# A retention head scales its values behind the third bank copy, and its rows are put together one unit later

## The chip, the cores and the metric

The kernel runs on one core of a Trainium2 chip. The metric is the device time of one execution in microseconds (us), the median of several runs. Beside it there is a profile of one execution.

## The reference

One layer of a decoder trunk: an RMS norm, one input projection into eight parts, a gated short convolution on four of them, retention on the other four, an output projection and a final RMS norm, all in fp32. Sixteen meta tokens stand ahead of the 2048 positions.

```python
D_MODEL, SEQ, N_META = 1024, 2048, 16      # D_CONV = D_RET = 512, 4 heads of 128

def short_conv_branch(h, b_gate, c_gate, conv_w):
    u = c_gate * h
    conv = causal_depthwise_conv(u, conv_w)             # width 3
    return b_gate * conv

def mixer_layer(h, norm_g, w_in, conv_w, ret_norm_g, w_out, pos):
    hn = rms_norm(h, norm_g)
    cx, cb, cc, cg, q, k, v, rg = jnp.split(hn @ w_in, 8, axis=-1)
    conv_out = short_conv_branch(cx, cb, cc, conv_w) * jax.nn.silu(cg)
    ...
    ret = head_group_norm(retention_chunkwise(rotary(q) * 128 ** -0.5, rotary(k), v), ret_norm_g)
    ret_out = ret * jax.nn.silu(rg)
    return h + jnp.concatenate([conv_out, ret_out], axis=-1) @ w_out

def reference(x, meta, ...):
    h = jnp.concatenate([meta, x], axis=1)
    h = mixer_layer(h, ...)
    return rms_norm(h, final_g)[:, N_META:]
```

`retention_chunkwise` works in chunks of 128 positions: masked scores q k^T times v inside a chunk, plus q times a 128x128 state carried from chunk to chunk with a fixed decay.

## The kernel before

**Rounds, units, quads.** The 2048 positions are done in two rounds of 1024 (two halves of 512). A round has eight units: four heads (0 to 3) and four conv groups (4 to 7), in the order of `UNITS`: round 0 begins with conv group 4 without the fast products, then heads 0 to 3, then 5 to 7; round 1 has heads 0 to 3 and then 4 to 7. After them come the output products. Each unit has two quads: a first one (k and v of a head, two of the conv's parts) and a second one (q and the gate rg, or the other two parts). A quad multiplies a 2x2 block of weights (blocks of 512 rows by 128 columns) with a 2x2 block of the moving rows by seven products (0 to 6) instead of eight. One product is 12 matmuls of L236: four slices of 128 rows, each as three matmuls, because each operand is split into a high part (`wh`, `mh`) and a rest (`wl`, `ml`). ACT casts `wh` (L112), DVE subtracts to get `wl` (L113), with three buffers of each. The sums of weight blocks that the seven products need are made in place by POOL (`sa`, `ra`: L121, L124, L151).

**Banks, copies and steps.** The products write into three PSUM banks: 0, 2, 4, 6 into `xb`, 1 into `yb`, 3 and 5 into `zb`. ACT copies a bank out (L243) after products 0, 2 and 3; these are the first, second and third bank copies, and product 5 overwrites the bank of the third. After each copy, `step()` calls the next of the quad's `steps`, whose instructions are to be placed behind that copy. `take` uses the finished banks on DVE.

**A head's second quad.** The matmuls of the retention need k and v turned from columns to rows. That is a transpose by DMA on 16-bit halves: a copy into planes by `part` (L678 on ACT, `pl`), the DMA (L671, `tr`), and a copy back (`v` by L766, `kd` by L757). The values `v` are then scaled by four small ACT instructions (L769), a factor for each chunk. Behind the first copy of the quad stand the splits of v and of half 0's k; behind the second `join(0)` (copy back and scaling of half 0's values) and the split of half 1's k; behind the third `join_keys(0)`; behind the quad the same for half 1. Then come the matmuls of the states (L798), the scores (L811, masked by DVE at L813 into `pm`) and the output (L821, L822), spread over the next unit's first quad.

**Turning the result.** A head's normalised output is turned back in two stages, each kept in `waiting`. Stage 0 (`turn`): ACT's copy L844, a transpose by DMA, silu of the gate (L847). It runs behind the first quad of the next unit. Stage 1 (`finish`), for each half of 512: ACT's copy L850 (`apart`), one product on DVE with gain and gate (L851, `qg`), and the store of the rows to DRAM (L506). `catch_up(1)` runs it behind the second quad of that next unit.

**What sets the order.** A scheduler gives each engine one fixed order of instructions when the kernel is built. It follows data and buffers, and the places that the code asks for with `issue_after`. In round 0, matmuls for the meta tokens (L456, L486, L494) are placed between those of the projection. SP issues nearly all DMAs, one queue in order: weight loads (L498), transposes (L671), stores (L506), and blocks of `w_out` with their sums (L427, L205).

Of the kernel before, what the change touches and what calls it, by code (L numbers as in the profile page):

```python
# [78 lines left out]
def hybrid_trunk(ctx: ExitStack, tc: tile.TileContext, t, out: bass.AP, chunk_decay):  # L79
# [5 lines left out]
    nc = tc.nc  # L85
# [40 lines left out]
    def load_raw(loads):  # L126
        tiles = []
        for load in loads:
            a = raw()
            load(a)  # L130
            tiles.append(a)
        return tiles
# [3 lines left out]
    def stationary(blocks):  # L136

        a11, a12, a21, a22 = blocks
        s1 = sb.tile([P, HB], F32, name="sa", tag="ra", bufs=RAW)

        def parts(src):
            hi = sb.tile([P, HB], F32R, name="wh", tag="wh", bufs=RING)
            lo = sb.tile([P, HB], F32R, name="wl", tag="wl", bufs=RING)
            split(hi, lo, src)
            return hi, lo

        w = [parts(a11), parts(a12)]
        add(nc.gpsimd, s1, a21, a22)
        sub(nc.gpsimd, a21, a11, a21)
        sub(nc.gpsimd, a11, s1, a11)  # L150
        summed[0] = nc.gpsimd.tensor_tensor(out=a12, in0=a12, in1=a11, op=ALU.subtract)  # L151
        w += [parts(a) for a in (a11, s1, a21)]
        fifth[0] = lowered[0]
        return w + [parts(a) for a in (a12, a22)]
# [70 lines left out]
    def quad(w, m, take, steps=()):  # L225


        steps = iter(steps)

        def product(i, bank, first):  # L230
            (wh, wl) = w[i]
            for kt in range(KH):
                ks = slice(kt * P, (kt + 1) * P)
                mh, ml = m[i][kt]
                for n, (a, b) in enumerate(((wl, mh), (wh, ml), (wh, mh))):
                    nc.tensor.matmul(  # L236
                        bank, a[:, ks], b, start=first and kt == 0 and n == 0, stop=kt == KH - 1 and n == 2,
                        skip_group_check=not first,
                    )

        def copy(bank):
            c = sb.tile([P, HB], F32, name="tc", tag="tc", bufs=COPIES)
            copied[0] = nc.scalar.copy(out=c, in_=bank)  # L243
            return c

        def step():
            with tc.issue_after(copied[0].ins):
                next(steps, lambda: None)()

        xb = ps_proj()  # L250
        product(0, xb, True)
        c = copy(xb)
        step()
        yb = ps_proj()
        product(1, yb, True)
        take(0, 0, yb, c)
        product(2, xb, False)
        u2 = copy(xb)
        step()
        zb = ps_proj()  # L260
        product(3, zb, True)
        c = copy(zb)
        step()
        product(4, xb, False)
        take(1, 1, xb, c)
        product(5, zb, False)
        take(0, 1, zb, u2)
        product(6, xb, False)
        take(1, 0, xb, None)
# [89 lines left out]
    def raw():  # L359
        return sb.tile([P, HB], F32, name="ra", tag="ra", bufs=RAW)  # L360
# [136 lines left out]
    def w_loads(n):  # L497
        return [lambda a, i=i: nc.sync.dma_start(a, t["w_in"][n, i]) for i in range(4)]  # L498
# [83 lines left out]
    def conv_group(g, r, m, f, blocks, ahead, steps=(), last=False):  # L582


        def go_on():
            next(factors_ahead[0], None)

        def behind(quad, *own):
            return [lambda n=n: (own[n](), go_on() if (quad, n) in steps else None) for n in range(3)]

        u = [gen("u") for _ in range(2)]
        rr, rr2 = ([a[:, j * HB : (j + 1) * HB] for j in range(2)] for a in f[:2])
        held = [None]

        def mul(eng, out, a, b):
            eng.tensor_tensor(out=out, in0=a, in1=b, op=ALU.mult)  # L596

        def take(i, j, pp, c):
            s = u[j][:, 2:]
            if c is None:  # L600
                mul(nc.vector, s, pp, s)
            elif i == 1:
                add(nc.vector, c, pp, c)
                held[0] = c
            else:
                add(nc.vector, s, pp, c)
                mul(nc.vector, s, s, rr2[j])
                if j == 1:
                    mul(nc.gpsimd, s, s, held[0])

        blocks, meta = blocks
        quad(stationary(blocks), m, take, behind(0, idle, idle, idle))
        catch_up(0)
        if meta:
            meta_carry(g, meta)
        carry(u, g, r)
        cs = [taps(u[j], g) for j in range(2)]
        gates = []

        def gated():  # L620
            j, c = gates.pop()
            nc.scalar.activation(c, c, AF.Silu)  # L622
            mul(nc.gpsimd, cs[j], cs[j], rr[j])
            mul(nc.gpsimd, cs[j], cs[j], c)

        def take(i, j, pp, c):
            if i == 0:
                add(nc.vector, c, pp, c)
                mul(nc.vector, c, c, rr[j])
                gates.append((j, c))  # L630
                if j == 1:
                    gated()
                return
            if c is not None:
                add(nc.vector, c, pp, c)
                pp = c
            taken[0] = nc.vector.tensor_tensor(out=cs[j], in0=pp, in1=cs[j], op=ALU.mult)  # L637

        n = 2 * (NG + g) + 1
        quad(stationary(load_raw(w_loads(n))), m, take, behind(1, idle, gated, idle))  # L640
        catch_up(1)
        blocks = ahead()
        def store():
            for j in range(2):
                store_mixed(r, j, g, cs[j])

        if last:
            kept.append(store)
        else:
            store()  # L650
        return blocks
# [12 lines left out]
    def halves(a):  # L664
        return a.bitcast(U16).rearrange("p (n two) -> p two n", two=2)

    def planes(a):
        return a.bitcast(U16).rearrange("p (two n) -> p two n", two=2)
# [16 lines left out]
    waiting = [[], []]  # L685

    def catch_up(stage):


        if waiting[stage]:  # L690
            with tc.issue_after(copied[0].ins):
                while waiting[stage]:
                    waiting[stage].pop(0)()

    def head(h, r, m, rot_t, f, turning, blocks, ahead, sums, first=(), between=((), idle, idle)):


# [3 lines left out]
        k, v, late = [None, None], [None, None], []  # L701
# [19 lines left out]
        if len(first) > 0:  # L721
            quad_plain(first[0], m, take)
        else:
            quad(stationary(blocks[0]), m, take, between[0])
            catch_up(0)
        between[1]()
        if to_cross:
# [27 lines left out]
        def join_keys(j):  # L755
            kt[j] = brief("kd")
            nc.scalar.copy(out=halves(kt[j]), in_=planes(across_k[j]))  # L757
# [6 lines left out]
        def join(j):  # L764
            a = gen("v")[:, :HB]
            nc.scalar.copy(out=halves(a), in_=planes(v[j]))  # L766
            for c in range(CH):
                cs = slice(c * P, (c + 1) * P)
                nc.scalar.mul(a[:, cs], a[:, cs], f[2][j][0][:, h, c : c + 1])  # L769
            v[j] = a  # L770

        def middle():
            join(0)
            split_keys(1)

        quad(stationary(load_raw(w_loads(2 * h + 1))), m, take, (split_late, middle, lambda: join_keys(0)))
        catch_up(1)
        with tc.issue_after(copied[0].ins):
            join(1)
            join_keys(1)  # L780
        between[2]()
        with tc.issue_after(queried[0].ins):
# [4 lines left out]
        with tc.issue_after(loaded[0].ins) if len(first) else nullcontext():  # L787
            blocks = ahead()
        states = [state[h]]
        vt = []  # L790
        for j in range(2):
# [4 lines left out]
            for c in range(CH - last):  # L796
                cs = slice(c * P, (c + 1) * P)
# [9 lines left out]
        for j in range(2):  # L807
            sc = ps_misc()
            for c in range(CH):
                cs = slice(c * P, (c + 1) * P)  # L810
# [8 lines left out]
            for c in range(CH):  # L819
                cs = slice(c * P, (c + 1) * P)  # L820
# [15 lines left out]
            for c in range(CH):  # L836
                cs = slice(c * P, (c + 1) * P)
# [133 lines left out]
    for r in range(NR):  # L971
        f = factors[r]
# [6 lines left out]
        if r == 0:  # L979
# [3 lines left out]
            def begin(half):  # L983
# [21 lines left out]
            m, b = moving(  # L1005
                load_x(r), gain_of, {(0, 0): lambda: begin(0), (0, KH - 1): lambda: begin(1), (0, KT - 1): normalise_meta}
            )
            first = [[p for a, p in w]]
            blocks = None, meta_products([a for a, p in w])
# [21 lines left out]
            between = (), idle, idle  # L1031
            later = prepare(load_x(1), sums_x, gain_of)
        else:
            m, b = moving(load_x(r), gain_of)
# [9 lines left out]
            between = (), rest_of_sums, idle  # L1044
            blocks = None, None
# [5 lines left out]
        for n, unit in enumerate(units):  # L1051
            following = units[n + 1] if n + 1 < len(units) else None
            rest = lambda: ahead(r, following, early=n == 0)
            if r + n == 0:
                blocks, completion = group_plain(unit - NG, m, f, blocks[1], first, late_parts, rest)
                special = (), completion
            elif unit < NG:
# [3 lines left out]
                blocks = head(unit, r, m, rot_t, f, turning, blocks, rest, sums, *(special if unit == 0 else ()))  # L1061
            else:
# [8 lines left out]
                blocks = conv_group(unit - NG, r, m, f, blocks, rest, FACTOR_STEPS.get(unit, ()) if r == 0 else (), r == 0 and following is None)  # L1071
# [4 lines left out]
    m, b = moving(load_w_out)  # L1076
# [42 lines left out]
```

## Time and profile before

| what | value |
|---|---|
| time, median of 3 runs | 870.76 us (869.86 to 871.42) |
| profiled execution, its time | 871.07 us |
| its span, first to last instruction | 869.3 us |
| granted TensorE clock | 0.998 |
| DMA | 129.51 MB, mean 149 GB/s |

Lines of the page's groups read: source line, engine, operation, output<-inputs, count | busy us in all, mean ns of one | idle us of the engine ahead of them and what ended it. Lines of the timeline read: start in us from the span's start, duration, engine, line, operation, operands, count, and in brackets idle time ahead of it with what ended it. PEld is the weight load of TensorE. Matmul durations overlap, since they are pipelined: the distance between two starts is what one costs. Lines of the view of waits read: the waiting engine and line, what it waited for, us in total, times, longest us.

### The profile page before, as it was taken

To read this page: it belongs to the slowest core of one execution; us is meant where nothing else is said; L and a number is where in the kernel's file an instruction comes from. 1 tells how busy PE (TensorE), PEld (TensorE's weight loads), DVE (VectorE), ACT (ScalarE), POOL (GpSimd) and SP (SyncE) were. 2 spreads that over 40 slices of the span, in tenths; PEclk is the share of its full clock that TensorE was granted. 3 is DMA by queue.
4 is the path that set the end of the run, shared out by engine and by line. 5 is a ranking of instruction groups with operands and counts; after the bars stand their busy time and mean duration, and the time that the engine had idled before them with its cause. 6 is when DMAs were issued, how large, how long until landed. Compare 5 with 4: busy or idle time off the path is not lost.

```text
span 869.3 us, 12705 instructions
## 1 busy us (share of the span) xinstructions
PE 857.9 (99%) x4216; PEld 704.7 (81%) x4216; DVE 722.5 (83%) x1194; ACT 497.9 (57%) x899; POOL 396.6 (46%) x286
## 2 busy tenths in 40 slices
PE   9999999999999999999999999999999999999996
PEld 6878887878787878788888888888888888788885
DVE  6899988888897977989789898988767799867663
ACT  8676548383845554848383747553333566545553
POOL 0663332322246654352233333355645445677773
PEclk9999999999999999999999999999999999999999
DMA  9724336363656633845264656647122584545441
GB/s 332 226 80 97 76 82 164 106 171 110 136 192 186 202 98 97 306 155 146 61 139 140 130 161 121 206 109 218 49 78 78 171 327 133 167 162 179 160 134 73
DMA packets 127219, 129.51 MB, mean 149 GB/s; under 512 B 58353, under 2 KB 75569, under 8 KB 127153
## 3 DMA queue, kind: packets, MB, share of 16 engines
q1 hardware_dynamic: 126576, 128.30, 50.0%
q8 instruction: 33, 0.54, 0.3%
q10 hardware_dynamic: 576, 0.40, 0.1%
q14 instruction: 34, 0.27, 0.1%
HBM read 90.91 MB, written 25.17 MB: 134 GB/s over the span
## 4 chain that ended last, share of the span: by engine, by line
PE 86%; DVE 3%; ACT 3%; issue 1%; DMA 1%; SPq 0%; POOLq 0%; POOL 0%; ACTq 0%; DVEq 0%
PE pj L236 73%; PE pj L293 5%; PE ms L822 2%; PE ms L811 2%; PE ms L821 2%; PE ms L798 2%; DVE ml L113 1%; PE ms L456 1%; ACT v L769 1%; ACT wh L112 1%; ACT v L766 1%; DVE wl L113 1%; DMA w<-in_w_out 1%; ACT tc L243 1%; DVE yo L121 0%
## 5 line engine op out<-in xcount | busy, mean ns | idle before, releaser
L236 PE MATMUL pj<-mh,wl 128*128 128x512 f32 x1008 | 397.2, 394 | 1.5 <-ACT tc L243 0.8
L236 PE MATMUL pj<-mh,wh 128*128 128x512 f32 x1008 | 393.0, 390 | 0.0
L236 PE MATMUL pj<-ml,wh 128*128 128x512 f32 x1008 | 392.7, 390 | 0.0
L112 ACT CAST wh<-ra 128x512 fp32r<-128x512 f32 x216 | 133.8, 620 | 245.2 <-PE pj L236 209.6
L113 DVE TENSOR_TENSOR wl<-ra,wh 128x512 fp32r<-128x512 f32 x216 | 194.4, 902 | 40.8 <-ACT wh L112 39.9
L236 PEld LDWEIGHTS pj<-mh,wl 128*128 128x128 f32 x1008 | 189.3, 188 | 45.5 <-ACT tc L243 3.9
L236 PEld LDWEIGHTS pj<-mh,wh 128*128 128x128 f32 x1008 | 189.3, 188 | 39.7
L236 PEld LDWEIGHTS pj<-ml,wh 128*128 128x128 f32 x1008 | 189.3, 188 | 37.5
L121 POOL TENSOR_TENSOR sa<-ra 128x512 f32<-128x512 f32 x36 | 53.0, 1473 | 104.7 <-DMA ra<-in_w_in 39.5
L124 POOL TENSOR_TENSOR ra<-sa,ra 128x512 f32<-128x512 f32 x36 | 53.9, 1497 | 91.8 <-DVE wl L113 88.8
L124 POOL TENSOR_TENSOR ra<-ra 128x512 f32<-128x512 f32 x36 | 59.1, 1643 | 49.4 <-PE ms L456 28.1
L151 POOL TENSOR_TENSOR ra<-ra 128x512 f32<-128x512 f32 x36 | 60.2, 1673 | 46.9 <-issue 37.1
L243 ACT COPY tc<-pj 128x512 f32<-128x512 f32 x108 | 62.7, 580 | 0.1
L293 PE MATMUL pj<-mh,mh 128*128 128x512 f32 x128 | 51.1, 400 | 0.7 <-ACT mh L115 0.6
L293 PE MATMUL pj<-mh,ml 128*128 128x512 f32 x128 | 50.1, 391 | 0.9 <-DVE ml L113 0.9
L293 PE MATMUL pj<-ml,mh 128*128 128x512 f32 x128 | 48.0, 392 | 0.0
L834 POOL TENSOR_TENSOR rp<-rs,neg_half 128x4 f32<-128x4 f32 x16 | 18.9, 1184 | 38.5 <-DVE rs L121 38.4
L596 POOL TENSOR_TENSOR c<-c,rr 128x512 f32<-128x512 f32 x14 | 24.9, 1778 | 24.3 <-DVE c L637 15.6
L897 DVE TENSOR_TENSOR yo<-pj,yo 128x512 f32<-128x512 f32 (+1 forms) x33 | 22.0, 671 | 16.2 <-PE pj L236 8.4
L908 POOL TENSOR_TENSOR z<-yo,final_g 128x512 f32<-128x512 f32 x16 | 26.8, 1675 | 18.6 <-DVE yo L897 18.6
L596 POOL TENSOR_TENSOR c<-c,tc 128x512 f32<-128x512 f32 x14 | 24.2, 1732 | 21.9 <-ACT tc L622 16.3
L112 ACT CAST wh<-sa 128x512 fp32r<-128x512 f32 x36 | 22.2, 617 | 15.0 <-PE pj L236 14.6
(153 smaller groups left out, 1218.9 us busy)
## 6 DMA issues: line engine op xcount, KB each, us to landing
ra<-in_w_in SPq DMA_DIRECT2D x126, 256.0 KB, 2.8
x<-in_xT SPq DMA_DIRECT2D x48, 256.0 KB, 4.9
w<-in_w_out SPq DMA_DIRECT2D x32, 256.0 KB, 4.7
ra<-mixed SPq DMA_DIRECT2D x32, 256.0 KB, 2.9
yo<-in_x SPq DMA_DIRECT2D x32, 256.0 KB, 4.9
ra<-in_x SPq DMA_DIRECT2D x16, 256.0 KB, 3.7
mixed<-c SPq DMA_DIRECT2D x16, 256.0 KB, 2.5
mixed<-qg SPq DMA_DIRECT2D x16, 256.0 KB, 2.4
```

What stands on the lines that cost most here:

```text
L112: nc.scalar.copy(out=hi, in_=src)
L113: lowered[0] = eng.tensor_tensor(out=lo, in0=src, in1=hi.bitcast(F32), op=ALU.subtract)
L121: eng.tensor_tensor(out=out, in0=a, in1=b, op=ALU.add)
L124: eng.tensor_tensor(out=out, in0=a, in1=b, op=ALU.subtract)
L151: summed[0] = nc.gpsimd.tensor_tensor(out=a12, in0=a12, in1=a11, op=ALU.subtract)
L236: nc.tensor.matmul(bank, a[:, ks], b, start=first and kt == 0 and n == 0, stop=kt == KH - 1 and n == 2, skip_group_check=not first,)
L243: copied[0] = nc.scalar.copy(out=c, in_=bank)
L293: nc.tensor.matmul(banks[i], a[:, ks], b, start=half + kt + n == 0, stop=half == 1 and kt == KH - 1 and n == 2,)
L596: eng.tensor_tensor(out=out, in0=a, in1=b, op=ALU.mult)
L834: nc.gpsimd.tensor_tensor(out=rp, in0=rs, in1=neg_half.rearrange("p (c a) -> p c a", a=1), op=ALU.pow)
L897: last[0] = nc.vector.tensor_tensor(out=y[:, cs], in0=pp[:, cs], in1=y[:, cs], op=ALU.add)
L908: nc.gpsimd.tensor_tensor(out=ys[i][j], in0=y, in1=final_g[:, j * HB : (j + 1) * HB], op=ALU.mult)
```

## The change

Two things are changed. A head's `join(0)` no longer scales half 0's values; the new `weigh(0)` does that behind the third bank copy instead of ahead of it, before `join_keys(0)`. And `catch_up(1)` is gone from the second quads of heads and conv groups; a new `finish_late` runs the waiting `finish` calls behind the first bank copy of the first quad of the unit after that. All instructions stay; a few lines move their numbers by some lines.

```diff
@@ conv_group
-        quad(stationary(blocks), m, take, behind(0, idle, idle, idle))
+        quad(stationary(blocks), m, take, behind(0, finish_late, idle, idle))
         catch_up(0)
...
         quad(stationary(load_raw(w_loads(n))), m, take, behind(1, idle, gated, idle))
-        catch_up(1)
@@
+    def finish_late():
+        while waiting[1]:
+            waiting[1].pop(0)()
@@ head
-            quad(stationary(blocks[0]), m, take, between[0])
+            quad(stationary(blocks[0]), m, take, between[0] or (finish_late,))
             catch_up(0)
...
         def join(j):
             a = gen("v")[:, :HB]
             nc.scalar.copy(out=halves(a), in_=planes(v[j]))
+            v[j] = a
+
+        def weigh(j):
             for c in range(CH):
                 cs = slice(c * P, (c + 1) * P)
-                nc.scalar.mul(a[:, cs], a[:, cs], f[2][j][0][:, h, c : c + 1])
-            v[j] = a
+                nc.scalar.mul(v[j][:, cs], v[j][:, cs], f[2][j][0][:, h, c : c + 1])
...
+        def late_middle():
+            weigh(0)
+            join_keys(0)
+
-        quad(stationary(load_raw(w_loads(2 * h + 1))), m, take, (split_late, middle, lambda: join_keys(0)))
-        catch_up(1)
+        quad(stationary(load_raw(w_loads(2 * h + 1))), m, take, (split_late, middle, late_middle))
         with tc.issue_after(copied[0].ins):
             join(1)
+            weigh(1)
             join_keys(1)
```

ACT, second quad of round 1's head 1, from the scalings ahead of the third bank copy (the first L243) to the cast ahead of the next unit's first one, before:

```order
L769 ACTIVATE v<-v,vk 128x128 x4
L112 CAST wh<-ra 128x512
L243 COPY tc<-pj 128x512
L757 COPY kd<-tr 128x2x512
L850 COPY apart<-across 128x2x512 x2
L112 CAST wh<-ra 128x512
L757 COPY kd<-tr 128x2x512
L112 CAST wh<-ra 128x512
L766 COPY v<-tr 128x2x512
L112 CAST wh<-ra 128x512
L769 ACTIVATE v<-v,vk 128x128 x4
L112 CAST wh<-sa 128x512
```

The same stretch now, and on to the next unit's first bank copy (the second L243) and the rows behind it. L766 is now L769, L769 is L775, L757 is L760, L850 is L859:

```order
L112 CAST wh<-ra 128x512
L243 COPY tc<-pj 128x512
L775 ACTIVATE v<-v,vk 128x128 x4
L760 COPY kd<-tr 128x2x512
L112 CAST wh<-ra 128x512
L760 COPY kd<-tr 128x2x512
L112 CAST wh<-ra 128x512 x2
L769 COPY v<-tr 128x2x512
L775 ACTIVATE v<-v,vk 128x128 x4
L112 CAST wh<-sa 128x512
L243 COPY tc<-pj 128x512
L859 COPY apart<-across 128x2x512 x2
```

The four scalings of half 0 stand behind the third copy, and the two copies of rows are out of this quad and in the next.

DVE, first quad of conv group 6 in round 0, around the `wl` of products 3 (from `sa`) and 4 (the next L113), before and now (L851 is now L860):

```order
L113 TENSOR_TENSOR wl<-sa,wh 128x512
L121 TENSOR_TENSOR u<-pj,tc 128x512
L113 TENSOR_TENSOR wl<-ra,wh 128x512
L596 TENSOR_TENSOR u<-u,rr_373 128x512
L113 TENSOR_TENSOR wl<-ra,wh 128x512 x2
```

```order
L113 TENSOR_TENSOR wl<-sa,wh 128x512
L860 SCALAR_TENSOR_TENSOR qg<-apart,ret_g,qg 128x512
L121 TENSOR_TENSOR u<-pj,tc 128x512
L860 SCALAR_TENSOR_TENSOR qg<-apart,ret_g,qg 128x512
L596 TENSOR_TENSOR u<-u,rr_373 128x512
L113 TENSOR_TENSOR wl<-ra,wh 128x512 x3
```

Both products of the last head's rows, and L596, now stand ahead of product 4's `wl`. In round 1, conv group 5 has the same rows.

PE, second quad of round 0's head 2, at the meta tokens' matmuls (L486, L456), before, between products 4 and 5, and then between 5 and 6:

```order
L236 MATMUL pj<-mh_709,wh 128x512
L486 MATMUL ms<-mk 128x128
L456 MATMUL ms<-ra,meta_s 16x128 x15
L236 MATMUL pj<-mh_244,wl 128x512
L236 MATMUL pj<-ml_245,wh 128x512
```

```order
L236 MATMUL pj<-ml_263,wh 128x512
L236 MATMUL pj<-mh_262,wh 128x512
L456 MATMUL ms<-ra,meta_s 16x128
L236 MATMUL pj<-mh_329,wl 128x512
L236 MATMUL pj<-ml_330,wh 128x512
```

Now, behind product 6, where before only the states' matmuls stood (L798, now L807):

```order
L236 MATMUL pj<-mh_368,wh 128x512
L486 MATMUL ms<-mk 128x128
L456 MATMUL ms<-ra,meta_s 16x128 x16
L807 MATMUL ms<-v,kd 128x128 x4
L236 MATMUL pj<-mh_123,wl 128x512
```

Three places between projection matmuls became one; in head 0 three became two.

## The prediction

> **What bounds the kernel now.** I read the shares of the page first, then what the chain that ended last is made of, then what TensorE waits for, and only then the places of those waits in the timeline.
>
> ```profile
> span 869.3 us, 12705 instructions
> PE 857.9 (99%) x4216; PEld 704.7 (81%) x4216; DVE 722.5 (83%) x1194; ACT 497.9 (57%) x899; POOL 396.6 (46%) x286
> ...
> PE 86%; DVE 3%; ACT 3%; issue 1%; DMA 1%; SPq 0%; POOLq 0%; POOL 0%; ACTq 0%; DVEq 0%
> ...
> PE pj L236 <- ACT tc L243: 0.8, 5, 0.2
> ```
>
> PE is busy 99% of the span and is 86% of the chain. So an edit that moves work on ACT or DVE is worth only the time in which PE stops, or the matmuls that it makes cheaper. The last row, from the view of waits, names such a stop: five times the projection's matmul waited for a bank copy. Here is one of them (second quad of round 1's head 1), first on ACT, then on PE.
>
> ```profile
> 445.00 1.36 ACT L766 COPY v<-tr 128x1024 uint16<-128x1024 uint16 x1
> 446.23 1.03 ACT L678 COPY pl<-kv 128x1024 uint16<-128x1024 uint16 x1
> 447.17 1.28 ACT L769 ACTIVATE v<-v,vk 128x128 f32<-128x128 f32 x4
> 448.35 0.61 ACT L112 CAST wh<-ra 128x512 fp32r<-128x512 f32 x1
> 448.86 0.58 ACT L243 COPY tc<-pj 128x512 f32<-128x512 f32 x1
> ...
> 450.56 2.56 ACT L850 COPY apart<-across 128x1024 uint16<-128x1024 uint16 x2
> ...
> 461.61 0.62 ACT L112 CAST wh<-ra 128x512 fp32r<-128x512 f32 x1 [1.61 <-PE pj L236]
> 465.98 0.62 ACT L112 CAST wh<-ra 128x512 fp32r<-128x512 f32 x1 [3.76 <-PE pj L236]
> ```
>
> ```profile
> 448.71 0.39 PE L236 MATMUL pj<-ml,wh 128*128 128x512 f32 x1
> 448.93 0.39 PE L236 MATMUL pj<-mh,wh 128*128 128x512 f32 x1
> 449.49 0.50 PE L236 MATMUL pj<-mh,wl 128*128 128x512 f32 x1 [0.17 <-ACT tc L243]
> 449.82 0.39 PE L236 MATMUL pj<-ml,wh 128*128 128x512 f32 x1
> ```
>
> Matmuls start 0.22 to 0.23 us apart (448.71 to 448.93; I use 0.227). Product 5 writes into the bank that the third copy reads, and this copy (448.86, 0.58 long) ends at 449.44: the matmul starts at 449.49 instead of 449.16. That is 0.33 lost, and the next one comes 0.33 after it instead of 0.227, 0.10 more, while the pipeline fills. So one stop costs 0.436. The copy is late because ACT's queue had no gap since 445.00: two layout copies and the four scalings of L769 stand ahead of it.
>
> **The change, part by part.** *The scalings go behind the third copy.* From 447.17 to 448.35 the queue gets 1.18 us shorter, so the copy would run from 447.68 to 448.26, 0.9 us ahead of the moment that PE wants the bank (449.16). Five stops go: 5 x 0.436 = 2.18 us. What would be late next? Round 1's head 0 has this shape by chance already (no rows to put together there, and its scalings behind the copy):
>
> ```profile
> 402.83 0.57 ACT L243 COPY tc<-pj 128x512 f32<-128x512 f32 x1
> ...
> 403.84 0.39 PE L236 MATMUL pj<-mh,wh 128*128 128x512 f32 x1
> 404.07 0.39 PE L236 MATMUL pj<-mh,wl 128*128 128x512 f32 x1
> ```
>
> The copy ends at 403.40, and PE goes from one product to the next in 0.23 us. So nothing else is late there, and I take the whole 2.18. Ends: 1.6, if 0.1 us were left at each stop through another late operand, and 2.2. The scaled values are wanted by the state's matmuls only, and those stand behind product 6.
>
> *ACT's two row copies (L850) leave that quad.* 2.56 us less at 450.56, and 2.56 more behind the first copy of a next quad. There ACT was idle for 1.61 and 3.76 us (rows at 461.61 and 465.98): hidden, cost nothing. If that cover were gone, the casts behind it would come up to 2.6 us later.
>
> *PE's small matmuls.* In round 0 the order changes where meta products are inserted between projection products: head 0 has one separate group fewer, head 2 two fewer (those groups now stand together). One such group in head 0:
>
> ```profile
> 93.47 0.39 PE L236 MATMUL pj<-mh,wh 128*128 128x512 f32 x1
> 93.79 0.39 PE L456 MATMUL ms<-ra,meta_s 128*16 128x128 f32 x2
> 94.11 0.50 PE L236 MATMUL pj<-mh,wl 128*128 128x512 f32 x1
> 94.44 0.39 PE L236 MATMUL pj<-ml,wh 128*128 128x512 f32 x1
> ```
>
> Going in costs 0.32 instead of 0.227, coming out 0.33 instead of 0.227: 0.09 + 0.10 = 0.20 a group. Three groups fewer are 0.6; a seam between two kinds of matmul inside one group may keep some of it. Ends 0.3 and 0.6, and I take 0.5.
>
> *DVE's two products of the rows (L851) leave the second quads.* The first conv unit behind the heads of round 0 loses its two, and the next unit's first quad, in which PE waits for DVE, profits:
>
> ```profile
> L851 DVE SCALAR_TENSOR_TENSOR qg<-apart,ret_g,qg 128x512 f32<-128x512 f32 x16 | 12.0, 753 | 7.8 <-ACT apart L850 7.8
> ```
>
> ```profile
> 295.59 0.39 PE L236 MATMUL pj<-mh,wh 128*128 128x512 f32 x1
> 295.95 0.50 PE L236 MATMUL pj<-mh,wl 128*128 128x512 f32 x1
> 296.29 0.39 PE L236 MATMUL pj<-ml,wh 128*128 128x512 f32 x1
> ...
> 298.81 0.39 PE L236 MATMUL pj<-mh,wl 128*128 128x512 f32 x1
> ```
>
> ```profile
> 295.21 0.69 DVE L113 TENSOR_TENSOR wl<-sa,wh 128x512 fp32r<-128x512 f32 x1
> 295.82 0.69 DVE L121 TENSOR_TENSOR u<-pj,tc 128x512 f32<-128x512 f32 x1
> 296.42 1.40 DVE L113 TENSOR_TENSOR wl<-ra,wh 128x512 fp32r<-128x512 f32 x1
> 297.74 1.79 DVE L596 TENSOR_TENSOR u<-u,rr 128x512 f32<-128x512 f32 x1
> ```
>
> Product 3 started 0.36 instead of 0.227 behind the matmul before it, just after its wl was ready (295.21 + 0.69 = 295.90), and refilled in 0.34: 0.24 us lost. DVE has 2 x 0.75 less to do before it now, so I take this stop as gone (ends 0 and 0.24).
>
> *They come back in the next first quad.* This is the giving back. In that same quad the order now puts both products, and L596 as well, ahead of product 4's wl, which here ended at 297.82 for a start at 298.81: 0.99 ahead. In round 1's second conv unit it is the same, ending at 601.16 for 602.15:
>
> ```profile
> 599.41 1.75 DVE L113 TENSOR_TENSOR wl<-ra,wh 128x512 fp32r<-128x512 f32 x1
> ...
> 602.15 0.39 PE L236 MATMUL pj<-mh,wl 128*128 128x512 f32 x1
> ```
>
> How long they take depends on POOL (the first two rows belong to round 0's quad, the others to round 1's):
>
> ```profile
> 295.98 1.29 POOL L121 TENSOR_TENSOR sa<-ra 128x512 f32<-128x512 f32 x1 [1.24 <-DMA mixed<-c]
> 297.35 1.63 POOL L124 TENSOR_TENSOR ra<-ra 128x512 f32<-128x512 f32 x1
> ...
> 599.31 1.30 POOL L121 TENSOR_TENSOR sa<-ra 128x512 f32<-128x512 f32 x1 [3.50 <-DMA ra<-in_w_in]
> 600.69 1.62 POOL L124 TENSOR_TENSOR ra<-ra 128x512 f32<-128x512 f32 x1
> ```
>
> The wl of 296.42 took 1.40 and not 0.69; it ended at 297.82, 0.55 behind POOL's end at 297.27. L596 ended at 299.53, again 0.55 behind POOL's 298.98. L121 on DVE, one of whose inputs is a PSUM bank, ran through in 0.69. The Trainium skill, page "SBUF — State Buffer", section "Who interferes with whom", says that a DVE instruction with two SBUF inputs and a GpSimd one that reads SBUF share a port pair, which whoever is first holds for its whole instruction while the other blocks. The trace agrees: 1.40 against 0.69. By that rule the moved products, whose inputs both lie in SBUF, can be blocked like this wl, so it speaks against the change; the sum would be by it the upper end that comes next.
>
> Upper end: the second moved product is held by the first POOL sum and ends at 297.82, L596 is held by the second until 299.53, and the wl follows 0.6 later, at 300.1. PE, 0.24 earlier, wants it at 298.57: a stop of 1.55 and 0.1 of refill. In round 1 the same walk ends at 602.31 + 0.55 + 0.6 = 603.5 for 602.15: 1.45. Lower end: 0 in both, if DVE is 1.5 us ahead and has both products done when POOL's first sum starts. POOL waited for a DMA there (1.24 and 3.50), so that sum comes no earlier. What is left then is one held instruction, 1.1 us, against 0.75 and 0.99 to spare. That is nearest to what I expect: 0.3 each, 0.6 together.
>
> *Queues.* SP issues the stores of the rows behind these products. Now they stand behind the loads that used to follow them, which can only go earlier, and ahead of three weight loads of the next unit. The rows are read back only by the output products. I take nothing for it: if those weight loads came a microsecond later, so would POOL's first sum, which waits for such loads (599.31), and it would fall behind the moved products. POOL's queue changes by a few swaps: nothing, and if a sum came a microsecond later, the wl behind it would carry it; that is no more than the ends above.
>
> Sum: 871.07 - 2.18 - 0.5 - 0.24 + 0.6 = 868.75 for the profiled execution (span 869.3, and 1.8 around it). It lies 0.31 above the median of 870.76, so I say 868.4.
>
> **The rivals.** *Given back.* Both wl stops come to somewhat over half of their upper ends, 1.9 together: 871.07 - 2.18 - 0.5 - 0.24 + 1.9 - 0.31 = 869.7, within 0.2% of before; full, 3.1, it is 870.9. For it: DVE has 83% of the span and stands packed in those quads, and POOL holds it there already. Against it: the group of L851 shows 7.8 us of idle DVE time that goes. The page named above describes how this case would come about.
>
> *Slower, at the scores.* In the first quad behind a head DVE also makes the masked scores (L813) for the output matmuls (L821), tightest in round 0's last head:
>
> ```profile
> 204.72 0.69 DVE L813 SCALAR_TENSOR_TENSOR pm<-ms,causal 128x512 f32<-128x512 f32 x1
> ...
> 205.76 0.38 PE L821 MATMUL ms<-v,pm 128*128 128x128 f32 x2
> ```
>
> 0.35 us to spare. The moved products stand ahead of L813 now. If both wait out POOL sums (1.4 each as above) and the 1.5 of relief was swallowed by filler work, DVE comes 1.3 later: 1.3 - 0.35 + 0.1 = 1.05 a quad. In the six quads that have both (three a round) it is 6.3: 868.4 + 6.3 = 874.7. It counts from 0.35 net lateness on, and at 0.65 it has eaten the gain (6 x 0.4). Against it: this place is the tightest, and DVE gets the relief half a unit before it pays.
>
> *It doesn't do what it says.* The third copy stays late, as something else fills ACT's queue ahead of it, and only the groups bring 0.3: about 870.5. The copy at 402.83 speaks against it.
>
> **How the numbers follow.** 0.2% (1.7 us) is about what a measurement of this kernel can tell from no change. Forecast 868.4 (its own range 867.5 to 869.2): chance 0.58. Given back, 869.7: 0.28. Nothing done, 870.5: 0.06. Slower at the scores: 0.08. Faster (under 869.0) is the forecast but for its upper tail, 0.52, and the lower tail of the second, 0.04: 0.56. Slower (over 872.5) is 0.07, the last case but for its mildest part. The rest, 0.37, is the same. The lowest that the bounds give is 871.07 - 2.2 - 0.6 - 0.24 - 0.31 = 867.7; with the scatter of the runs 867.2. Up to 870.8 the range holds nearly all of the second case and the third, and leaves out the last.
>
> **What would show it.** Right: the wait of L236 for the bank copy falls from five rows to none; DVE's idle time at the moved product is well below 7.8. Wrong: PE rows that wait for wl (L113) at the start of product 4 in the second conv unit of either round, over 0.5 us each, or L821 waiting for the masked scores behind heads.

## The result, and the profile after

The changed kernel takes 869.39 us (median of 21 runs, 868.07 to 871.11) beside 871.32 us of the kernel before (21 runs on the same chip): ratio 0.9978, 95% interval 0.9972 to 0.9985. That is 1.9 us less, where 2.4 us less were forecast. A second set of runs gave 0.9987 (0.9979 to 0.9996). Its profiled execution took 868.33 us. The page after, and what PE waited for (view of waits; L906 is a line of the output products):

```profile
span 866.5 us, 12699 instructions
...
PE 855.4 (99%) x4216; PEld 705.1 (81%) x4216; DVE 725.7 (84%) x1194; ACT 497.8 (57%) x899; POOL 394.6 (46%) x286
...
PE pj L236 <- DVE wl L113: 0.7, 2, 0.5
...
PE pj L236 <- DVE yo L906: 0.5, 1, 0.5
```

PE is still the bound. The row of L236 behind L243, the third bank copy, is gone. A row behind `wl` (L113) stands in its place: two waits, one of 0.54 in conv group 6 of round 0, shown below, and one of 0.18 in round 0's head 1. The span fell by 2.8 us, more than the median, and part of that isn't the change. Here are the first matmul of head 0's second quad in round 0, and the first of the last conv quad before the output products, before and after:

```profile
75.75 0.39 PE L236 MATMUL pj<-mh,wl 128*128 128x512 f32 x1
...
686.47 0.39 PE L236 MATMUL pj<-mh,wl 128*128 128x512 f32 x1
```

```profile
74.75 0.39 PE L236 MATMUL pj<-mh,wl 128*128 128x512 f32 x1
...
684.25 0.39 PE L236 MATMUL pj<-mh,wl 128*128 128x512 f32 x1
```

1.0 us had been won by 75 us, ahead of the first place that the change touches. In the changed kernel's second trace that matmul starts at 76.24, in all other traces of this study between 75.1 and 77.0, so the opening scatters by more than the change brings. Between the two rows lie 610.72 us before and 609.50 after: 1.22 less, and 1.22 less again in the changed kernel's second trace. I call this time **the stretch** and compare kernels by it as well as by their medians. A **stop** is the time by which a matmul starts later than 0.227 behind the one before it, and its **refill** is what the next matmul loses in the same way. The brackets of the timeline show the idle part of a stop alone, 0.16 less.

Where it came from, in the trace. ACT and PE at the second quad of round 1's head 1, as shown of before:

```profile
443.75 1.36 ACT L769 COPY v<-tr 128x1024 uint16<-128x1024 uint16 x1
444.99 1.04 ACT L677 COPY pl<-kv 128x1024 uint16<-128x1024 uint16 x1
445.93 0.62 ACT L112 CAST wh<-ra 128x512 fp32r<-128x512 f32 x1
446.45 0.58 ACT L243 COPY tc<-pj 128x512 f32<-128x512 f32 x1
446.93 1.28 ACT L775 ACTIVATE v<-v,vk 128x128 f32<-128x128 f32 x4
```

```profile
447.69 0.39 PE L236 MATMUL pj<-mh,wh 128*128 128x512 f32 x1
447.91 0.39 PE L236 MATMUL pj<-mh,wl 128*128 128x512 f32 x1
```

The third copy ends at 447.03, 0.88 ahead of product 5's first matmul, which follows the one before it in 0.22 us. All five such stops went: 0.45 to 0.48 each by the starts of the products, refill included, 2.32 us in all.

The meta matmuls of round 0's head 2 are one group now:

```profile
188.63 0.39 PE L236 MATMUL pj<-mh,wh 128*128 128x512 f32 x1
188.95 0.48 PE L486 MATMUL ms<-mk 16*128 16x128 f32 x2
189.36 1.07 PE L456 MATMUL ms<-ra,meta_s 128*16 128x128 f32 x32
190.36 1.16 PE L807 MATMUL ms<-v,kd 128*128 128x128 f32 x8
191.27 0.48 PE L236 MATMUL pj<-mh,wl 128*128 128x512 f32 x1
```

Head 2 won 0.57 by it and head 0, with one place fewer, 0.21: 0.78 together.

And where part of it went. The first quad of conv group 6 in round 0, PE, DVE and POOL:

```profile
296.48 0.39 PE L236 MATMUL pj<-mh,wh 128*128 128x512 f32 x1
297.41 0.47 PE L236 MATMUL pj<-mh,wl 128*128 128x512 f32 x1 [0.54 <-DVE wl L113]
```

```profile
292.50 0.75 DVE L860 SCALAR_TENSOR_TENSOR qg<-apart,ret_g,qg 128x512 f32<-128x512 f32 x1
293.17 0.69 DVE L121 TENSOR_TENSOR u<-pj,tc 128x512 f32<-128x512 f32 x1
293.77 1.19 DVE L860 SCALAR_TENSOR_TENSOR qg<-apart,ret_g,qg 128x512 f32<-128x512 f32 x1
294.88 1.78 DVE L596 TENSOR_TENSOR u<-u,rr 128x512 f32<-128x512 f32 x1
```

```profile
293.08 1.32 POOL L121 TENSOR_TENSOR sa<-ra 128x512 f32<-128x512 f32 x1 [1.66 <-DVE wl L113]
294.48 1.63 POOL L124 TENSOR_TENSOR ra<-ra 128x512 f32<-128x512 f32 x1
```

The second moved product ends at 294.96, 0.56 behind POOL's first sum (294.40), and L596 at 296.66, 0.55 behind the second (296.11). The `wl` behind them is late, and product 4 starts 0.93 instead of 0.227 behind the matmul before it. The same stop in round 1, at 599.81, cost 0.24 and 0.08 of refill. Over the whole program the moved product is dearer than it was (before: 12.0 us, 753 ns each):

```profile
L860 DVE SCALAR_TENSOR_TENSOR qg<-apart,ret_g,qg 128x512 f32<-128x512 f32 x16 | 19.5, 1218 | 0.0
```

It no longer waits for ACT (0.0 against 7.8 us), and it lasts 7.5 us longer: what it gave back in waiting it pays nearly in full behind POOL. Eleven of the 16 take 1.18 to 1.79 us and end 0.55 behind an instruction of POOL; the other five take 0.74 or 0.75. Before, one of the 16 ended so, and it took 0.80.

### The profile page after: what moved, and what is told of

It reads as the page before. It is cut to its first block, busy times and chain, and to the rows that moved or that the text cites. A ratio compares the mean times of both kernels' runs of the same rounds, so it can differ in the third digit from the quotient of the medians.

```text
span 866.5 us, 12699 instructions
## 1 busy us (share of the span) xinstructions
PE 855.4 (99%) x4216; PEld 705.1 (81%) x4216; DVE 725.7 (84%) x1194; ACT 497.8 (57%) x899; POOL 394.6 (46%) x286
## 4 chain that ended last, share of the span: by engine, by line
PE 78%; DVE 6%; issue 1%; ACT 0%; POOL 0%; POOLq 0%; DVEq 0%
PE pj L236 66%; PE pj L293 5%; PE ms L831 1%; PE ms L820 1%; PE ms L830 1%; PE ms L807 1%; DVE wl L113 1%; PE ms L456 1%; DVE ml L113 1%; DVE ml L116 0%; DVE yo L121 0%; DVE yo L906 0%; DVE yo L941 0%; ACT n L407 0%; DVE tc L121 0%
## 5 line engine op out<-in xcount | busy, mean ns | idle before, releaser
L236 PE MATMUL pj<-mh,wl 128*128 128x512 f32 x1008 | 396.0, 393 | 1.3 <-DVE wl L113 0.7
L236 PE MATMUL pj<-mh,wh 128*128 128x512 f32 x1008 | 393.1, 390 | 0.0
L236 PE MATMUL pj<-ml,wh 128*128 128x512 f32 x1008 | 392.9, 390 | 0.0
L236 PEld LDWEIGHTS pj<-mh,wl 128*128 128x128 f32 x1008 | 189.3, 188 | 43.1 <-issue 1.5
L113 DVE TENSOR_TENSOR wl<-ra,wh 128x512 fp32r<-128x512 f32 x216 | 192.4, 893 | 36.6 <-ACT wh L112 35.2
L236 PEld LDWEIGHTS pj<-mh,wh 128*128 128x128 f32 x1008 | 189.3, 188 | 39.4
L236 PEld LDWEIGHTS pj<-ml,wh 128*128 128x128 f32 x1008 | 189.3, 188 | 38.1
L124 POOL TENSOR_TENSOR ra<-sa,ra 128x512 f32<-128x512 f32 x36 | 51.3, 1424 | 81.8 <-DVE wl L113 79.6
L243 ACT COPY tc<-pj 128x512 f32<-128x512 f32 x108 | 62.6, 580 | 0.1
L596 POOL TENSOR_TENSOR c<-c,rr 128x512 f32<-128x512 f32 x14 | 25.7, 1834 | 22.2 <-DVE c L637 14.1
L906 DVE TENSOR_TENSOR yo<-pj,yo 128x512 f32<-128x512 f32 (+1 forms) x33 | 22.0, 671 | 15.9 <-PE pj L236 8.5
L847 DVE TENSOR_SCALAR pm<-ms,mv,rp 128x128 f32<-128x128 f32 x64 | 21.9, 403 | 11.8 <-POOL rp L843 11.8
```

The lines of the kernel that those rows point to most:

```text
L113: lowered[0] = eng.tensor_tensor(out=lo, in0=src, in1=hi.bitcast(F32), op=ALU.subtract)
L124: eng.tensor_tensor(out=out, in0=a, in1=b, op=ALU.subtract)
L236: nc.tensor.matmul(bank, a[:, ks], b, start=first and kt == 0 and n == 0, stop=kt == KH - 1 and n == 2, skip_group_check=not first,)
L847: nc.vector.tensor_scalar(out=y[:, cs], in0=o[:, cs], scalar1=mv[:, c, 0:1], scalar2=rp[:, c, :], op0=ALU.subtract, op1=ALU.mult,)
L906: last[0] = nc.vector.tensor_tensor(out=y[:, cs], in0=pp[:, cs], in1=y[:, cs], op=ALU.add)
```

## The experiments

Each kernel was timed beside the kernel before, unless it says that there is one profiled run only. "Stretch" is against before's 610.72.

**The scalings alone.** From the kernel before, only this:

```diff
+            weigh(0)          # behind the third copy, no longer in join(0)
             join_keys(0)
```

> Kernel before with the scalings of half 0 behind the third bank copy, rows put together where they were before. Theory (the gain is the third bank copy, which comes 1.2 us earlier): no wait of L236 for L243 in the heads' second quads, 5 x 0.436 = 2.2 us less, one place of meta matmuls fewer in head 0 (0.2), no stop at product 4 of the quads of conv group 6 (round 0) and 5 (round 1), since nothing is moved there: about 2.4 us less than before, ratio 0.9973. Rival (the rows' copies on ACT and products on DVE made the quad late): nothing gained, ratio 1.000, and the five waits stay.

870.83 us, ratio 1.001 (1.0001 to 1.0018), stretch 0.0. Neither was right as a whole: the five waits went as the theory said, and yet nothing was won, as the rival said. In round 1 a new wait stands at the end of each of these quads (PE first, then DVE; in this kernel L857 and L858 are the rows' copy and product):

```profile
453.87 1.05 PE L805 MATMUL ms<-v,kd 128*128 128x128 f32 x8
455.51 0.47 PE L236 MATMUL pj<-mh,wl 128*128 128x512 f32 x1 [0.58 <-DVE wl L113]
```

```profile
451.21 0.75 DVE L858 SCALAR_TENSOR_TENSOR qg<-apart,ret_g,qg 128x512 f32<-128x512 f32 x1 [0.83 <-ACT apart L857]
451.88 0.68 DVE L121 TENSOR_TENSOR qg<-pj,tc 128x512 f32<-128x512 f32 x1
452.48 0.74 DVE L858 SCALAR_TENSOR_TENSOR qg<-apart,ret_g,qg 128x512 f32<-128x512 f32 x1
...
454.67 1.29 DVE L113 TENSOR_TENSOR wl<-ra,wh 128x512 fp32r<-128x512 f32 x2
```

DVE waits for the rows' copy, does the rows, and comes to the next quad's first `wl` at 454.67. PE is there by then, since it no longer stopped at the third copy: three stops of 0.73 to 0.75 and 0.08 of refill (455.51, 501.40, 547.62), more than the three of 0.46 that they replace. The stretch of 0.0 is a sum: 0.57 of it was won at round 1's start, where PE waits for an `ml` of the moving rows. There the traces of this study differ by up to 0.7 us, and no experiment was made on it; without it this kernel lost 0.56.

**The rows alone.** From the changed kernel:

```diff
             join(0)
+            weigh(0)
...
-            weigh(0)          # in late_middle
```

> Changed kernel with the scalings of half 0 back ahead of the third bank copy; only the rows move. Theory: the five waits for the third copy stay (0.33 and 0.11 each), the stops at product 4 of round 0's conv group 6 and round 1's conv group 5 are there (0.8 and 0.3), the stop at product 3 of the former goes (0.24): 0.9 us more than before, ratio 1.001. Rival (the rows carry the gain): ratio 0.998.

871.9 us, 1.002 (1.0012 to 1.0029), stretch 0.96 longer, close to the 0.9 of the theory. In part that is luck: the two conv quads gave 1.00 of it, a third copy that is now late in head 2 of round 0 as well gave 0.32 and conv group 5 of round 0 gave 0.21, neither of them foreseen, and round 1's start took 0.64 back. The waits for the copy are there, six now, and the two for `wl` of the moved rows too:

```profile
PE pj L236 <- ACT tc L243: 1.1, 6, 0.2
...
PE pj L236 <- DVE wl L113: 0.7, 2, 0.5
```

Neither part wins anything by itself. Together they do.

**The scalings, and no rows at all.** The kernel with the scalings alone, without the two instructions that put the rows together (one profiled run):

```diff
-    nc.scalar.copy(out=halves(apart), in_=planes(across))
-    nc.vector.scalar_tensor_tensor(out=sg[j], in0=apart, scalar=ret_g[:, h : h + 1], in1=sg[j], ...)
```

> The kernel with only the scalings moved, and the rows' copies on ACT and products on DVE left out (the gates are stored unscaled). Theory (the stops of 0.8 at product 0 behind the heads of round 1, which that kernel had, come from the rows' work in the second quad): they go, the five waits for the third copy stay gone, and nothing stops at product 4 of the conv groups' quads. Rival (the scalings themselves make wl late there): the stops of 0.8 stay.

869.16 us. The stops at product 0 are gone, and those for the third copy in the heads too; the stretch is 2.73 shorter, 0.38 of it at round 1's start. In the same place PE goes straight on:

```profile
454.49 1.05 PE L805 MATMUL ms<-v,kd 128*128 128x128 f32 x8
455.30 0.48 PE L236 MATMUL pj<-mh,wl 128*128 128x512 f32 x1
```

So it was the rows' work in the second quad that ate the scalings' gain.

**The last head's rows, elsewhere.** From the changed kernel, one line in the conv groups: the rows behind the third bank copy of the first quad (`behind(0, idle, idle, finish_late)`); behind the second one (`behind(0, idle, finish_late, idle)`); the same in round 1 only; or back behind the second quad:

```diff
         quad(stationary(load_raw(w_loads(n))), m, take, behind(1, idle, gated, idle))
+        catch_up(1)
```

> Changed kernel, but the conv groups put the last heads' rows together behind the third bank copy of their first quad instead of the first; heads as changed. Order: both products (L860) behind the wl of product 4. Theory: the stops at product 4 (0.8 and 0.3) go, and nothing is late in their place: 1.1 us less than the changed kernel, ratio to before 0.9966. Rival (DVE has too much to do there wherever it is put): a stop of the same size at product 5 or 6, ratio 0.998.

> Changed kernel, but the last head's rows are put together behind the second quad of the first conv group, as before the change (one line is put back); the rows of the heads before it stay a unit later. Theory: the stops at product 4 of the next first quad (0.8 and 0.3) go and the one at product 3 there (0.24) may come back: 0.9 to 1.1 us less than the changed kernel, ratio 0.9967. Rival (the stops come from POOL's sums being earlier or later, not from the moved products): the stops stay, 0.998.

> Changed kernel, but both rounds' conv groups put the last head's rows together behind the second bank copy of their first quad. Order: both products (L860) stand between the wl of product 4 and that of product 5. Theory (the stops come from what stands ahead of product 4's wl, held by POOL): the stops at product 4 go, 1.1 us less than the changed kernel; ACT's two copies stand ahead of the third bank copy now, so a wait for that copy of up to 0.5 could come in their place. Ratio to before 0.9968. Rival (any place in that quad costs the same): 0.998.

> Changed kernel; the conv groups put the last head's rows together behind the second bank copy in round 1 only, behind the first in round 0 as changed. Theory: the stop at product 4 of round 1's conv group 5 goes (0.35), the one of round 0 stays: 0.35 less than the changed kernel, ratio to before 0.9976. Rival: no change against the changed kernel.

| the last head's rows | ratio | stretch | stop, round 0 | stop, round 1 |
|---|---|---|---|---|
| behind the first copy (the change) | 0.9978, 0.9987 | -1.22, -1.22 | 0.70 at product 4 | 0.24, 0.32 at product 4 |
| behind the third copy | 0.9991 (0.9981 to 1.0) | -1.34 | 1.2 a quad later | none |
| behind the second copy | 0.9979 (0.9970 to 0.9988) | -1.63 | 0.62 at product 5 | none |
| second copy, round 1 only | 0.9982 (0.9973 to 0.9991) | -1.71 | 0.69 at product 4 | none |
| behind the second quad | 0.9983 (0.9974 to 0.9991) | -1.45 | 0.57 at the next quad | none |

(Stops by the starts of the matmuls, without refill.) In round 1 the theory held: with the products out of the way of product 4's `wl`, no stop is left. In round 0 the stop at product 4 went as well where the rows were moved, but one of 0.6 to 1.2 turned up elsewhere, as the rivals had it, though not always where they had it. So the three kernels that move the rows in both rounds win 0.1 to 0.4 over the changed kernel in the stretch (0.8 in a second trace of the second-copy kernel, below), and not the 0.9 to 1.1 that were forecast. Behind the second copy it was the wait that its expectation named, the third copy behind ACT's two row copies (PE, then ACT):

```profile
300.48 0.50 PE L236 MATMUL pj<-mh,wl 128*128 128x512 f32 x1 [0.46 <-ACT tc L243]
```

```profile
295.66 2.59 ACT L859 COPY apart<-across 128x1024 uint16<-128x1024 uint16 x2
...
299.35 0.60 ACT L112 CAST wh<-ra 128x512 fp32r<-128x512 f32 x1
299.86 0.57 ACT L243 COPY tc<-pj 128x512 f32<-128x512 f32 x1
```

Behind the third copy it was a bank copy of the next quad, in front of which ACT waited for DVE (PE, then ACT). DVE had done the rows 8 us earlier; that they made it late there was not tried by itself:

```profile
312.10 0.50 PE L236 MATMUL pj<-mh,wl 128*128 128x512 f32 x1 [1.05 <-ACT tc L243]
```

```profile
309.72 1.34 ACT L519 ACTIVATE c<-u,conv_w 128x512 f32<-128x512 f32 x2 [3.39 <-DVE u L596]
```

In the one with the rows back behind the second quad it was a `wl`, at the next quad's first product (287.41). The medians differ too little to order these kernels among themselves, and so does the stretch: two traces of the second-copy kernel differ in it by 0.36.

**Work, or held by POOL?** The changed kernel with the moved product on 64 of its 512 columns (one profiled run):

```diff
-    out=sg[j], in0=apart, ..., in1=sg[j],
+    out=sg[j][:, :64], in0=apart[:, :64], ..., in1=sg[j][:, :64],
```

> Changed kernel with the product L860 on 64 of 512 columns (the other columns of the rows stay without gain and gate: left out of the computation). DVE order in the conv groups' quads as in the changed kernel. Theory (the instructions are held by POOL's sums and end 0.55 behind them): the narrow product takes 0.15 us free of POOL but around 1 us or more where a POOL sum runs, and product 4 still stops for 0.5 to 0.8 in round 0, since L596 is held all the same. Rival (it is the 2 x 0.75 us of DVE work): the narrow products take 0.15 everywhere and the stop is gone.

Round 0's conv group 6, DVE, POOL and PE:

```profile
294.45 0.28 DVE L860 SCALAR_TENSOR_TENSOR qg<-apart,ret_g,qg 128x64 f32<-128x64 f32 x1
294.65 0.68 DVE L121 TENSOR_TENSOR u<-pj,tc 128x512 f32<-128x512 f32 x1
295.25 1.15 DVE L860 SCALAR_TENSOR_TENSOR qg<-apart,ret_g,qg 128x64 f32<-128x64 f32 x1
296.33 0.68 DVE L596 TENSOR_TENSOR u<-u,rr 128x512 f32<-128x512 f32 x1
296.93 2.99 DVE L113 TENSOR_TENSOR wl<-ra,wh 128x512 fp32r<-128x512 f32 x3
```

```profile
295.03 1.29 POOL L121 TENSOR_TENSOR sa<-ra 128x512 f32<-128x512 f32 x1 [1.65 <-DVE qg L860]
296.40 1.76 POOL L124 TENSOR_TENSOR ra<-ra 128x512 f32<-128x512 f32 x1
```

```profile
298.86 0.47 PE L236 MATMUL pj<-mh,wl 128*128 128x512 f32 x1 [0.42 <-DVE wl L113]
```

The same eighth of the work takes 0.28 us (0.15 was expected), and 1.15 when it starts 0.22 behind POOL's sum: it ends with that sum (296.40 against 296.32). Product 4 still stopped, 0.58 at 298.86 against 0.70 in the changed kernel. What held it was not L596, as I had expected, which got through in 0.68, but the `wl` behind it (three took 2.99). In round 1 the stop did go, though the narrow product was held there too (1.31): the rival has half a point. The Trainium skill, page "SBUF — State Buffer", section "Who interferes with whom", has the rule that a DVE instruction with two SBUF inputs and a GpSimd one that reads SBUF exclude each other for a whole instruction. The trace agrees: 1.15 against 0.28 at the same size. This kernel's time (870.22 us, stretch 0.77 shorter than before) says nothing on the question: the meta matmuls of head 2 are placed otherwise in it, which costs 0.37, and two quads in round 1's heads lost 0.36 and 0.35.

**A better place.** Round 1 behind the second copy; in round 0 the last head's rows one quad later still, behind the first copy of conv group 6's second quad. The second-copy kernel ran once more beside it.

```diff
+        ... behind(0, *((idle, finish_late, idle) if r else (finish_late if g == 1 else idle, idle, idle)))
+        ... behind(1, idle if r else finish_late if g == 2 else idle, gated, idle)
```

> Changed kernel; in round 1 the last head's rows behind the second bank copy of the conv group's first quad, in round 0 one quad later still: behind the first copy of conv group 6's second quad. Theory (each place has its own slack; that second quad of round 0 has more of it): no stop at product 4 or 5 of round 0's conv group 6 (0.8 gone) nor of round 1's conv group 5 (0.3 gone), so 1.1 us less than the changed kernel, ratio to before 0.9967. Rival (as with the second copy, a stop of about 0.6 moves to the new place): 0.9975.

> The kernel with the last head's rows behind the second bank copy of the conv groups' first quads, once more on the same chip as the next later place: ratio to before 0.9976 (it gave 0.9979), with the wait for the third copy of 0.6 in round 0 that its first trace showed.

868.11 us, ratio 0.997 (0.9958 to 0.9982), stretch 3.18 shorter; the second-copy kernel 868.21 us, 0.9974 (0.9962 to 0.9985), stretch 1.99 shorter. One wait of L236 behind `wl` is left, head 1's, of which below:

```profile
PE pj L236 <- DVE wl L113: 0.3, 1, 0.3
```

Against the changed kernel the stretch is 2.0 shorter: the 1.1 of the two stops, and 0.66 at round 1's start, where PE's wait for an `ml` was 0.48 instead of 1.19 us (no experiment was made on that). Both stops that it was to remove are gone, as the theory said, although the second of the two products of round 0 was held in its new place too (1.20 us): it was early enough there. Its median is the lowest measured here; its interval overlaps that of the second-copy kernel, and of the 1.19 by which its stretch is the shorter, 0.66 are from round 1's start.

**The changed kernel once more.**

> The changed kernel once more, as the measure for the next two on the same chip: ratio to before 0.998; trace as before, with the stops at product 4 (0.8 and 0.3) and at head 1 of round 0 (0.4).

869.73 us, 0.9987. All its stops are there: 0.34 at head 1, 0.70 and 0.32 at product 4.

## Why the prediction was right, and where it was not

- *The third bank copy.* 2.18 us forecast, 2.32 in the trace. The size was right, and what was said of it was not: I took it for what moving the scalings is worth by itself, and the rows' leaving ACT's queue for "hidden, cost nothing". The scalings alone won 0.0. The step that failed is the question "what would be late next?", which I answered from round 1's head 0, where the next unit's first `wl` had no rows ahead of it. That quad has neither the scalings nor the rows; it showed what the two together would bring, and not what one would.
- *PE's small matmuls.* 0.5 forecast, 0.78 measured, of which 0.57 in head 2. It was undersized; even the upper end, 0.6, was.
- *The stop at product 3 in round 0's conv group 6.* Forecast to go, and gone (0.24).
- *The giving back.* Place and engines were right; 0.3 and 0.3 were forecast, 0.78 and 0.32 came. The step that failed is "that sum comes no earlier". Measured against PE at product 4, DVE was 1.4 to 1.5 us earlier than before, as hoped. But POOL's first sum was earlier too, by 1.0 us in round 0, where it waited for DVE's `wl` (293.08) and no longer for a DMA, and by 1.2 us in round 1, where it still waited for its load. So in both rounds the walk that I called the upper end is what happened, second product held by the first sum, L596 by the second, only from an earlier start. Round 1, DVE and POOL:

```profile
596.13 1.22 DVE L860 SCALAR_TENSOR_TENSOR qg<-apart,ret_g,qg 128x512 f32<-128x512 f32 x1
```

```profile
595.51 1.29 POOL L121 TENSOR_TENSOR sa<-ra 128x512 f32<-128x512 f32 x1 [3.65 <-DMA ra<-in_w_in]
```

  The product ends at 597.35, 0.55 behind POOL's sum, and L596 at 599.05, 0.54 behind the next one. I had one held instruction left over, and there were two. That round 1 came to 0.32 for the 0.3 forecast is luck.
- *Not foreseen.* In head 1's second quad of round 0 product 2 waits for a `wl`:

```profile
127.86 0.47 PE L236 MATMUL pj<-mh,wl 128*128 128x512 f32 x1 [0.18 <-DVE wl L113]
```

```profile
121.39 1.37 DVE L847 TENSOR_SCALAR pm<-ms,mv,rp 128x128 f32<-128x128 f32 x4 [1.12 <-POOL rp L843]
...
127.03 0.68 DVE L113 TENSOR_TENSOR wl<-ra,wh 128x512 fp32r<-128x512 f32 x1
```

  0.43 with its refill. The order now has the normalising of a head's second half, with its wait for POOL, ahead of this `wl`, where before it stood behind it. Every kernel with the scalings moved has this stop (0.18 to 0.48), the one without has not. Another 0.36 was lost over conv group 5's two quads in round 0, where the order splits 16 meta matmuls into 11 and 5 instead of 12 and 4. All kernels with 11 and 5 lost 0.21 to 0.36 there, all with 12 and 4 0 to 0.16; why, was not tried by itself. Both places were to be read from the order; I had weighed neither.
- *The sum.* In the stretch: -2.32 - 0.78 - 0.24 + 0.78 + 0.32 + 0.43 + 0.36 = -1.45; small shifts between heads make up the rest to -1.22. I had -2.32 for the same terms. The rival "given back" had -1.02, so the trace lies nearer to it than to the forecast. But of the 1.89 given back only 1.10 are at the two places that the forecast and this rival named; the rest is what neither foresaw.
- *The time.* 869.39 lies 0.99 above the forecast of 868.4, just outside the forecast's own range (867.5 to 869.2) and inside the wide one (867.2 to 870.8), which takes in most of the rival "given back". 0.56 of the 0.99 is the kernel before, which took 871.32 beside it and not 870.76; the other 0.43 is a gain that came out smaller, 1.93 for 2.36.
- *The signs.* The five waits went and DVE's idle time at the moved product fell to 0.0, as the forecast said. The sign of being wrong, a wait for `wl` at product 4 of over 0.5 us in each case, showed in round 0 (0.54) and not in round 1.
- *The rival at the scores.* It did not come: no matmul waited for the masked scores. But the tightest place, in round 1's conv group 4, has 0.22 us to spare now; before, the tightest was the 0.35 of round 0's last head.

## What to carry to other kernels

When an engine in order holds up the bound, moving one thing out of its way is worth the stop only if the next thing that the bound needs is early enough as well: look for it on the next engine, at the end of the same stage. And judge a place for work of DVE that reads two SBUF tensors by what POOL does then (0.75 us free and up to 1.79 behind POOL here), and by how early PE's next operand is: in the second-copy kernel both products of round 0 ran free (0.75) and PE stopped for a bank copy instead, in the better place one was held (1.20) and PE did not stop. Where a kernel's opening scatters more than the effect, compare the traces over the stretch that the edit can reach.

## What the runs showed of the hardware

A held DVE product of 512 columns ends 0.55 us behind POOL's sum (eleven of 16 in the changed kernel), and one of 64 columns 0.08 behind it (both times). Two traces of one kernel agree in the length of the stretch to 0.01 us for the changed kernel (1.22 less than before, twice), and differ by 0.36 for the second-copy kernel (1.63 and 1.99), in which head 1's stop was 0.48 once and 0.18 once. The start of head 0's second quad lay between 74.75 and 77.00 us in the traces, 2.25 apart, more than the 1.9 us that the change brings.
